# Convolutions placed 100 instructions sooner, and the output's late products tile by tile, in a hybrid decoder layer

## The chip, the cores and the metric

The kernel runs on one core of a Trainium2 chip. A core has a matrix engine (TensorE, PE in the profile), a vector engine (VectorE, DVE), a scalar engine (ScalarE, ACT), a general engine (GpSimd, POOL), and queues that issue transfers (SyncE's, SP, among them). Each engine takes its instructions in the order in which the program lists them for it; semaphores make one engine wait for another. Matrix products are written to PSUM, a small memory that VectorE and ScalarE then read; the other operands lie in SBUF.

The metric is the device time of one execution in microseconds (us). The time before is 1002.07 us, the median of three runs (1002.04 to 1004.28).

## The reference

The program computes one layer on 512 tokens and 16 meta tokens (528 positions) of width 1024, in float32:

```python
u = rmsnorm(h, mix_norm_w[i])
proj = u @ w_in[i]                       # pool | z | xbc | dt | gates
...
y_pool = pool_mixer(u_pool, ...) @ w_pool_up[i]
y_ssd = mamba2_branch(z, xbc, dt_raw, ...) @ w_ssd_out[i]
h = h + (gate_pool * y_pool + gate_ssd * y_ssd) @ w_o[i]
v = rmsnorm(h, mlp_norm_w[i])
hid = jax.nn.relu(v @ w_ff1[i])
h = h + (hid * hid) @ w_ff2[i]
out = rmsnorm(h, final_norm_w)
```

The part that the change touches lies in `mamba2_branch`. A causal depthwise convolution of width 4, with bias and Silu, runs over xbc (4096 channels, 32 tiles of 128 channels):

```python
y = b
for k in range(CONV_WIDTH):
    y = y + xp[:, k:k + seqlen] * w[k]
xbc = jax.nn.silu(y)
```

Its result is split into x (2048 channels, 32 heads), B and C (1024 each, 8 groups of 128 states). A chunked scan (chunks of 128) makes y per group from x, B, C and dt; y is multiplied by silu(z), normed per group, and multiplied by `w_ssd_out`.

## The kernel before

Every matrix product is made from a high and a low part of each operand: high times high, high times low, low times high, summed in PSUM. A weight block (128 x 1024) is loaded to `raw`, cast to its high part `whi` on ScalarE (line 111), and its low part `wlo` is the difference, made on VectorE (line 113). These go through pools of four buffers for `whi` and `wlo`.

The scan runs over eight groups g = 0 to 7. `ssd(g)` is a generator that makes the scan of group g in steps; `group_proj(g + 1)` is a generator that makes the projections of the next group: two tiles for B and C (`bt`, `ct`), two for x (`xc`), and z. `weave` takes a step of the one and a step of the other in turn, and between them steps of some side work. For group 7 there is no next group; its partner is `out_part`, which makes the middle part of the output product: for each of 8 output tiles d, the terms k = 8 to 13 of `w_ssd_out` (y of groups 4 to 6).

The steps of `ssd(g)`: transposes of B and x, the scaled x (`xdt`, `xdd`) and the decay matrix `abc` (subtract on ScalarE, line 638, and VectorE, line 641; Exp on ScalarE, lines 644 and 645); then C times B, its mask (`cbm`, line 658), the chunk states (`st`, lines 667 to 673) and the product of mask and decay (line 676); then for each half of the channels `po` (line 685) and `py` (line 691), and y on VectorE (lines 694 to 698); then the squares, their sums (`png`, lines 709 and 710), the root and its reciprocal (lines 712 and 714), and y in high and low parts (`yh`, `yl`, lines 718 to 722).

The convolution of a channel tile is `conv(dst, src, ct)`: one ScalarE instruction (bias and the weight of the newest position, line 437), three VectorE instructions (the three older positions, line 440), then Silu on ScalarE (line 442). For most tiles `src` is the PSUM tile `px` that the projection has just written (lines 215 and 218); for the x tiles of groups 4 to 7 it is a pair of SBUF tiles. PSUM tiles of this size (`px`, `pz`, `pgp`, `pso`, `psp`) come from one pool with two buffers; a tile can be taken when the last reader of the one two places before is done.

The order of instructions on each engine isn't written out by hand. A planner takes, whenever an engine is free in its model, the ready instruction with the smallest place; the place is the position in the trace of the Python program, and `tc.high_priority(100)` lets a block of instructions count as 100 places earlier. Before the change it is used for weight blocks (`block`, `pair_operands`). Buffers are given out in the same walk.

In `out_part`, `part` makes the products of one tile d for some k, and `add` copies the PSUM tile to SBUF (ScalarE, line 868) and adds it to `acc_d` in DRAM with a transfer issued by GpSimd (line 869). The staging tile comes from a pool of two buffers. Tiles d = 0 and 1 get k = 8 to 11 first; their k = 12 and 13 (y of group 6, not ready as early) come later, in three rounds over both tiles (line 880). Then the tiles d = 2 to 7 follow, each whole. `weight_sums_at` issues transfers on GpSimd that are paced by small copies (`seen`, line 797).

After the scan, `pool_pair` multiplies by pool weights (line 998, its copies at lines 1004 to 1014), the merge and the MLP follow (lines 1077 to 1670).

Of the kernel before, what the change touches and what calls it, by code (L numbers as in the profile page):

```python
# [11 lines left out]
AF = mybir.ActivationFunctionType  # L12
ALU = mybir.AluOpType
# [21 lines left out]
V_MIX, V_BG, V_PS, V_CW, V_CB, V_DS, V_SN, V_MN, V_DTB, V_AL = (  # L35
    0, 8, 24, 32, 160, 192, 208, 224, 232, 233)
# [28 lines left out]
def kernel(ctx: ExitStack, tc, xT, x, w, fx, f1, f2, vec, fnw, out):  # L65
    nc = tc.nc
    act, dve, pe, pool = nc.scalar, nc.vector, nc.tensor, nc.gpsimd
# [19 lines left out]
    def block_tiles():  # L87
        b = nblk[0]
        nblk[0] += 1
        return (b, raw_tile(f"raw{b}"),  # L90
                wp.tile([P, 1024], F32R, tag="whi", name=f"whi{b}"),
                wp.tile([P, 1024], F32R, tag="wlo", name=f"wlo{b}"))

    def block_load(t, c):
        nc.sync.dma_start(t[1][:, c], w[t[0], :, c])
# [5 lines left out]
    def after(*ins):  # L101
        st = ExitStack()
        for i in ins:
            if i is not None:
                st.enter_context(tc.issue_after(i.ins))
        return st
# [36 lines left out]
    def mm3s(ps, pairs, first=True, last=True):  # L143

        for n, ((ah, al), (bh, bl)) in enumerate(pairs):
            pe.matmul(ps, ah, bh, start=first and n == 0, stop=False)  # L146
            pe.matmul(ps, ah, bl, start=False, stop=False)
        for n, ((ah, al), (bh, bl)) in enumerate(pairs):
            pe.matmul(ps, al, bh, start=False, stop=last and n == len(pairs) - 1)
# [16 lines left out]
    def col(off, i, n=P):  # L166
        return vs[:n, off + i : off + i + 1]
# [25 lines left out]
    def psum2(name):  # L193
        return psa.tile([P, 1024], F32, tag="mm", name=name)

    def psum1(name):
        return psb.tile([P, 512], F32, tag="s", name=name)
# [150 lines left out]
    for t, name in ((rsh, "dgh"), (rsl, "dgl")):  # L348
        d = pre.tile([NT, 6, NT], F32R, tag="sq", name=name, bufs=2)
# [16 lines left out]
    def dtile(name):  # L366
        return dp.tile([P, W], F32, name=name)

    v, e, s, s2, pl, dt, acs = (dtile(n) for n in ("dv", "de", "ds", "ds2", "dpl", "ddt", "dacs"))
# [21 lines left out]
    for c in (slice(0, P), slice(P, W)):  # L391
        n = c.stop - c.start
# [41 lines left out]
    def conv(dst, src, ct):  # L434
        n = dst.shape[-1]
        e = src.shape[-1] - n
        act.activation(dst, src[:, e:], AF.Identity, bias=col(V_CB, ct), scale=col(V_CW, ct * 4 + 3))
        for j in range(1, 4):
            o = max(0, j - e)
            dve.scalar_tensor_tensor(dst[:, o:], src[:, e + o - j : e + n - j],  # L440
                                     col(V_CW, ct * 4 + 3 - j), dst[:, o:], op0=ALU.mult, op1=ALU.add)
        silu = act.activation(dst, dst, AF.Silu)
        mark[0] = dst[:, :1]
        if ct < 16:
            x_ready[ct // 2] = silu
# [84 lines left out]
    def group_proj(g, cur, gate=None):  # L530
# [4 lines left out]
        def plain(dst, t, skip):  # L535
            if first and (dst is bt or dst is ct):
                view = viewB if dst is bt else viewC
            else:
                runs, view = wide(psum2(f"px{g}_{t}"), skip)
                proj(runs, block(), X if first else U)  # L540
            conv(dst, first_raw(t, view, skip) if first else view, t)
# [205 lines left out]
    def staged(name):  # L747
        return gtp.tile([P, SEQ], F32, tag="gt", name=name)
# [90 lines left out]
    def out_part():  # L839

        def get(n):
            t = block_tiles()
            block_load(t, slice(0, 1024))

            with after(b_meta[G - 1] if n == 1 else None):
                cast = act.copy(t[2], t[1])
            if n == 1:
                late_cast[0] = cast
            with tc.issue_after(x_decayed[G - 1].ins) if n == 1 else nullcontext():
                dve.tensor_tensor(t[3], t[1], t[2].bitcast(F32), op=ALU.subtract)  # L850
            return t

        def pieces():
            blocks = [get(0), get(1)]
            for n in range(6):
                t = blocks[n] if n < 2 else get(n)
                for j in range(NK):
                    c = slice(j * P, (j + 1) * P)
                    yield t[2][:, c], t[3][:, c]

        un = pieces()

        def part(ps, d, ks):
            mm3s(ps, [(next(un), ys[k]) for k in ks], ks[0] == 8, ks[-1] == 13)

        def add(ps, d):
            o = staged(f"sp{d}")
            act.copy(o, ps)
            nc.gpsimd.dma_start(acc_d[d], o, accum_op=ALU.add)


        ps = [psum2(f"psp{d}")[:, :SEQ] for d in range(2)]
        for d in range(2):
            part(ps[d], d, range(8, 12))
            yield
        late = [[(next(un), ys[k]) for k in (12, 13)] for d in range(2)]
        for o in ((0, 0), (1, 0), (0, 1)):
            for d in range(2):
                for n, (a, b) in enumerate(late[d]):
                    pe.matmul(ps[d], a[o[0]], b[o[1]], start=False, stop=o[1] == 1 and n == 1)  # L880
            yield
        for d in range(2):
            add(ps[d], d)
        for d in range(2, NK):
            ps = psum2(f"psp{d}")[:, :SEQ]
            part(ps, d, range(8, 14))
            add(ps, d)
            yield
# [39 lines left out]
    for g in range(G):  # L928
        nxt = group_tiles(g + 1) if g + 1 < G else None
        fill = [group_proj(g + 1, nxt, GATE_AT.get(g))] if nxt else [out_part()]  # L930
        if g == 4:
            fill = [out_half()] + fill
        weave(ssd(g, cur), fill, 2 if g == 4 else 1, weight_sums_at(SETS_AT[g], PIECES.get(g, 12)),
              [sums_of_u(g)] if g in SUMS_AT else [])
        cur = nxt
# [115 lines left out]
    for d in range(NK):  # L1051
        ps = psum1(f"psl{d}")
# [108 lines left out]
    for n, d in enumerate(MERGE):  # L1161
# [9 lines left out]
        ps = psum2(f"pup{d}")[:, :SEQ]  # L1171
# [389 lines left out]
    for c in range(NC - 1):  # L1561
        z, e = c == 0, c == NC - 2

        n = 2 * c + 3
# [78 lines left out]
    for t in range(4):  # L1643
        T, st = t // 2, slice((t % 2) * P, (t % 2 + 1) * P)
        n = 0
        for half in range(2):
            parts = [(0, 512)] if half == 0 or t < 3 else [(0, 256), (256, 256)]
            for a, m in parts:
                ps = p2v[t] if T == 0 and half == 0 else lastp[:, 512:] if a else (
                    lastp[:, :512] if (t, half) == (3, 0) else psum1(f"pl{t}_{half}"))  # L1650
                ps = ps[:, a : a + m]
# [15 lines left out]
                src = ps  # L1667
                if not a:
                    src = ht[:, t, cs]
# [162 lines left out]
```

## Time and profile before

| | before |
|---|---|
| median of 3 runs | 1002.07 us (1002.04 to 1004.28) |
| the profiled execution, its own time | 1003.26 us |
| its span | 1001.6 us |
| granted TensorE clock | 0.999 |
| busy: TensorE, weight loads, VectorE, ScalarE, GpSimd | 989.0, 873.4, 804.2, 602.9, 121.9 us |

The span runs from the first to the last instruction of one profiled execution. In a row of a group or of a timeline stand: the start in us (timeline) and the duration, the engine (PEld is TensorE's load of a stationary operand, a name with q its queue), the line of the program, the operation, the tiles written and read, the shape, and in brackets or behind the bar the idle time of the engine just before, with what ended it. A timeline merges neighbours (x8 is eight of them). In a row of stretches stand the stretch, its length and the busy time of PE, PEld, DVE, ACT and POOL with the number of instructions, then the granted clock, the share of the DMA engines and GB/s. The ends of matmuls are modelled: one of 512 columns is shown as 0.39 us, though the next can start 0.23 us after it.

### The profile page before, as it was taken

Reading aid. Unit: us, or ns where it says so; the run is one execution under the profiler, and the core shown is the slowest. Engines: PE = TensorE matmul, PEld = TensorE weight load, DVE = VectorE, ACT = ScalarE, POOL = GpSimd, SP = SyncE. Lnnn points to the kernel's source line nnn. Section 1 sums busy time; section 2 is a strip of 40 time slices with the busy share of each in tenths; the row PEclk is TensorE's granted clock in tenths of the full one; section 3 lists DMA queues with packets and bytes.
Section 4 is the critical chain, followed back from the end, with each engine's and each line's share of the span. In section 5 each row is a group of like instructions: output and inputs, shape, how many; then the busy total and the mean of one; then the engine's idle time right before and its main releaser. Section 6 shows DMA issues by size and latency. Waiting matters only on the chain.

```text
span 1001.6 us, 15673 instructions
## 1 busy us (share of the span) xinstructions
PE 989.0 (99%) x6035; PEld 873.4 (87%) x6035; DVE 804.2 (80%) x1162; ACT 602.9 (60%) x855; POOL 121.9 (12%) x215
## 2 busy tenths in 40 slices
PE   9999999999999999999999999999999999999997
PEld 7889898989889999978898888888889999999986
DVE  7977997879855888978789667876988878888885
ACT  7657749494924658574345443377666666656654
POOL 0010321211212312223200001121000000000000
PEclk9999999999999999999999999999999999999999
DMA  7374868676798849678823732889354464454332
GB/s 245 89 254 140 265 182 238 195 192 199 221 262 265 232 122 278 211 161 172 286 68 127 252 101 77 259 232 323 88 197 149 142 194 138 157 185 151 129 106 84
DMA packets 61803, 184.52 MB, mean 184 GB/s; under 512 B 7072, under 2 KB 8416, under 8 KB 60704
## 3 DMA queue, kind: packets, MB, share of 16 engines
q1 hardware_dynamic: 39456, 109.00, 33.3%
q0 software_dynamic: 18240, 67.51, 26.4%
q10 hardware_dynamic: 4032, 7.00, 1.9%
q8 instruction: 47, 0.77, 0.3%
q14 instruction: 28, 0.23, 0.1%
HBM read 173.13 MB, written 58.59 MB: 231 GB/s over the span
## 4 chain that ended last, share of the span: by engine, by line
PE 84%; DVE 7%; ACT 4%; DMA 3%; issue 1%; SPq 0%; ACTq 0%; DVEq 0%
PE px L1451 8%; PE px L215 7%; PE alpha L1519 6%; PE pz L215 6%; PE px L1454 4%; PE px L218 4%; PE pgp L215 3%; PE alpha L1522 3%; PE pz L218 3%; PE pgs L215 3%; DMA raw<-in_w 2%; PE pqx L506 2%; PE py L691 2%; PE pgp L218 2%; PE pso L146 1%; PE wo_alpha L1213 1%
## 5 line engine op out<-in xcount | busy, mean ns | idle before, releaser
L113 DVE TENSOR_TENSOR wlo<-raw,whi 128x1024 fp32r<-128x1024 f32 (+2 forms) x88 | 102.2, 1171 | 45.0 <-ACT whi L111 29.7
L111 ACT CAST whi<-raw 128x1024 fp32r<-128x1024 f32 (+2 forms) x88 | 87.2, 1012 | 64.0 <-DMA raw<-in_w 15.8
L215 PE MATMUL px<-uh,whi 128*128 128x264 f32 (+1 forms) x320 | 81.1, 291 | 0.0
L218 PE MATMUL px<-ul,whi 128*128 128x264 f32 (+1 forms) x320 | 78.7, 284 | 0.0
L1226 DVE TENSOR_TENSOR ht<-ht,alpha 128x1024 f32<-128x1024 f32 x35 | 42.7, 1220 | 29.1 <-PE alpha L1519 29.1
L215 PEld LDWEIGHTS px<-uh,whi 128*128 128x128 f32 x320 | 60.5, 189 | 1.1 <-issue 0.9
L1149 ACT CAST shi<-rawf 128x1024 fp32r<-128x1024 f32 x42 | 44.2, 1053 | 28.0 <-PE alpha L1522 18.4
L218 PEld LDWEIGHTS px<-ul,whi 128*128 128x128 f32 x320 | 60.2, 188 | 0.4 <-issue 0.2
L1519 PE MATMUL alpha<-shi,hh 128*128 128x512 f32 x140 | 55.3, 395 | 0.7 <-DVE ht L1226 0.6
L1522 PE MATMUL alpha<-shi,hl 128*128 128x512 f32 x140 | 54.7, 391 | 0.0
L1150 DVE TENSOR_TENSOR slo<-rawf,shi 128x1024 fp32r<-128x1024 f32 x42 | 51.2, 1219 | 0.6 <-ACT shi L1149 0.6
L1454 PE MATMUL px<-vsl,shi 128*128 128x256 f32 x192 | 47.4, 280 | 0.0
L1451 PE MATMUL px<-vsh,shi 128*128 128x256 f32 x192 | 47.4, 281 | 0.0
L215 PE MATMUL pz<-uh,whi 128*128 128x512 f32 x112 | 43.8, 391 | 1.7 <-DVE xc L440 1.7
L218 PE MATMUL pz<-ul,whi 128*128 128x512 f32 x112 | 43.6, 390 | 0.0
L215 PE MATMUL px<-uh,wlo 128*128 128x264 f32 (+1 forms) x320 | 42.0, 283 | 0.0
L215 PEld LDWEIGHTS px<-uh,wlo 128*128 128x128 f32 x320 | 40.0, 188 | 0.0
L1519 PE MATMUL alpha<-slo,hh 128*128 128x512 f32 x140 | 37.4, 389 | 0.0
L1451 PEld LDWEIGHTS px<-vsh,shi 128*128 128x128 f32 x192 | 36.2, 188 | 0.9
L1454 PEld LDWEIGHTS px<-vsl,shi 128*128 128x128 f32 x192 | 36.1, 188 | 0.9
L1454 PE MATMUL px<-vl,shi 128*128 128x256 f32 x144 | 36.1, 283 | 0.0
L1451 PE MATMUL px<-vh,shi 128*128 128x256 f32 x144 | 36.0, 282 | 0.0
(599 smaller groups left out, 3068.3 us busy)
## 6 DMA issues: line engine op xcount, KB each, us to landing
raw<-in_w SPq DMA_DIRECT2D x96, 512.0 KB, 4.6
f_t<-in_f POOLq DMA_DIRECT2D x38, 512.0 KB, 7.5
f_s<-in_f POOLq DMA_DIRECT2D x26, 512.0 KB, 7.0
b<-in_f SPq DMA_DIRECT2D x21, 512.0 KB, 4.4
rawf<-in_f SPq DMA_DIRECT2D x36, 256.0 KB, 3.0
rawf<-f_t SPq DMA_DIRECT2D x36, 256.0 KB, 3.1
abc<-acs_d POOLq DMA_DIRECT2D x8, 1024.0 KB, 8.3
f_t<-f_t POOLq DMA_DIRECT2D x12, 512.0 KB, 6.7
```

What stands on the lines that cost most here:

```text
L111: act.copy(hi[:, c], raw[:, c])
L113: dve.tensor_tensor(lo[:, c], raw[:, c], hi[:, c].bitcast(F32), op=ALU.subtract)
L215: pe.matmul(o, wt, rhs[0][k][:, c], start=part == 0 and k == 0, stop=part == 1 and k == NK - 1)
L218: mm[0] = pe.matmul(o, wt, rhs[1][k][:, c], start=False, stop=False)
L506: at = pe.matmul(o, wk, f[k][0], start=start and not low and k == 0, stop=stop and low == 1 and k == 3, skip_group_check=True)
L1149: splits.append((act.copy(hi, src), dve.tensor_tensor(lo, src, hi.bitcast(F32), op=ALU.subtract)))
L1150: dve.tensor_tensor(lo, src, hi.bitcast(F32), op=ALU.subtract)))
L1226: added[0] = dve.tensor_tensor(o, o, src, op=op)
L1451: pe.matmul(ps, m, f[k][0], start=start and not low and k == 0, stop=stop and low == 1 and k == 3, skip_group_check=True)
L1454: pe.matmul(ps, m, f[k][1], start=False, stop=False, skip_group_check=True)
L1519: pe.matmul(ps[t], hh[:, p, seg, st], m, start=bool(first and not low and p == 0), stop=bool(last and low and p == 1), skip_group_check=True)
L1522: pe.matmul(ps[t], hl[:, p, seg, st], m, start=False, stop=False, skip_group_check=True)
```

## The change

Two edits. In `conv`, the ScalarE instruction and the three VectorE instructions stand in a block that counts as 100 places earlier; the Silu stays outside. In `out_part`, the late products run tile by tile instead of round by round: the six matmuls of tile 0, then its copy and its transfer in a block of 100 places earlier, a yield, then the same for tile 1. There are two yields where there were three, and the copies of both tiles no longer stand ahead of the step of tile 2.

```diff
     def conv(dst, src, ct):
         n = dst.shape[-1]
         e = src.shape[-1] - n
-        act.activation(dst, src[:, e:], AF.Identity, bias=col(V_CB, ct), scale=col(V_CW, ct * 4 + 3))
-        for j in range(1, 4):
-            o = max(0, j - e)
-            dve.scalar_tensor_tensor(dst[:, o:], src[:, e + o - j : e + n - j],
-                                     col(V_CW, ct * 4 + 3 - j), dst[:, o:], op0=ALU.mult, op1=ALU.add)
+        with tc.high_priority(100):
+            act.activation(dst, src[:, e:], AF.Identity, bias=col(V_CB, ct), scale=col(V_CW, ct * 4 + 3))
+            for j in range(1, 4):
+                o = max(0, j - e)
+                dve.scalar_tensor_tensor(dst[:, o:], src[:, e + o - j : e + n - j],
+                                         col(V_CW, ct * 4 + 3 - j), dst[:, o:], op0=ALU.mult, op1=ALU.add)
         silu = act.activation(dst, dst, AF.Silu)
...
         late = [[(next(un), ys[k]) for k in (12, 13)] for d in range(2)]
-        for o in ((0, 0), (1, 0), (0, 1)):
-            for d in range(2):
+        for d in range(2):
+            for o in ((0, 0), (1, 0), (0, 1)):
                 for n, (a, b) in enumerate(late[d]):
                     pe.matmul(ps[d], a[o[0]], b[o[1]], start=False, stop=o[1] == 1 and n == 1)
+            with tc.high_priority(100):
+                add(ps[d], d)
             yield
-        for d in range(2):
-            add(ps[d], d)
         for d in range(2, NK):
             ps = psum2(f"psp{d}")[:, :SEQ]
             part(ps, d, range(8, 14))
```

## The prediction

> **What bounds the kernel now.** I read the page first (engines, chain of waits, costliest groups), then busy time in stretches, then the groups of TensorE kept apart by shape, and last the timelines around the two places they name.
>
> ```profile
> span 1001.6 us, 15673 instructions
> ...
> PE 989.0 (99%) x6035; PEld 873.4 (87%) x6035; DVE 804.2 (80%) x1162; ACT 602.9 (60%) x855; POOL 121.9 (12%) x215
> ...
> PE 84%; DVE 7%; ACT 4%; DMA 3%; issue 1%; SPq 0%; ACTq 0%; DVEq 0%
> ...
> L215 PE MATMUL pz<-uh,whi 128*128 128x512 f32 x112 | 43.8, 391 | 1.7 <-DVE xc L440 1.7
> ```
> ```profile
> L146 PE MATMUL psp<-yh,whi 128*128 128x512 f32 x44 | 17.5, 397 | 1.4 <-ACT sp L868 1.4
> ```
> ```profile
> 60.00:110.00 50.00, 48.31 (x339) 43.93 (x338) 38.41 (x63) 29.72 (x42) 7.61 (x16) 1.00 0.66 220
> 110.00:315.00 205.00, 205.00 (x1330) 183.07 (x1329) 160.37 (x246) 134.65 (x182) 44.68 (x81) 1.00 0.77 219
> 315.00:430.00 115.00, 114.88 (x833) 106.62 (x832) 93.60 (x143) 72.84 (x104) 28.23 (x49) 1.00 0.73 211
> 430.00:450.00 20.00, 18.33 (x104) 14.61 (x103) 17.72 (x31) 17.27 (x26) 3.27 (x5) 1.00 0.66 163
> 450.00:500.00 50.00, 49.60 (x272) 42.61 (x271) 39.88 (x56) 21.60 (x29) 16.05 (x25) 1.00 0.86 230
> ```
>
> TensorE is busy 989.0 of 1001.6 us, and 84% of the chain of waits is its own work. So the change can win only what TensorE loses. Between 60 and 500 us that is 50 - 48.31 = 1.69, then 0.00, 0.12, 1.67 and 0.40 us, 3.88 in all. Two places hold 3.1 of it, and both have a name in the groups: the z product waits 1.7 us for the last step of a convolution (L440), and the output part waits 1.4 us for a copy out of PSUM (L868). These are the two helpers that the diff touches. VectorE stands at 80% of the span, and at 17.72 of 20 us around the second place, so whatever is put ahead there pushes something else back.
>
> **The first stall.** The rows come from the timelines of TensorE, ScalarE and VectorE.
>
> ```profile
> 101.35 2.09 PE L215 MATMUL px<-uh,wlo 128*128 128x264 f32 x16
> 105.13 0.47 PE L215 MATMUL pz<-uh,whi 128*128 128x512 f32 x1 [1.69 <-DVE xc L440]
> 108.88 1.98 PE L215 MATMUL pz<-uh,wlo 128*128 128x512 f32 x8
> ```
> ```profile
> 95.32 0.79 ACT L437 ACTIVATE xc<-px,vs 128x528 f32<-128x528 f32 x1
> ...
> 101.59 1.05 ACT L111 CAST whi<-raw 128x1024 fp32r<-128x1024 f32 x1 [1.58 <-PE px L218]
> ```
> ```profile
> 95.90 1.22 DVE L113 TENSOR_TENSOR wlo<-raw,whi 128x1024 fp32r<-128x1024 f32 x1
> ...
> 101.14 0.76 DVE L440 SCALAR_TENSOR_TENSOR xc<-px,vs,xc 128x527 f32<-128x527 f32 x1
> 101.82 1.22 DVE L113 TENSOR_TENSOR wlo<-raw,whi 128x1024 fp32r<-128x1024 f32 x1
> 102.95 0.76 DVE L440 SCALAR_TENSOR_TENSOR xc<-px,vs,xc 128x526 f32<-128x526 f32 x1
> ...
> 104.23 0.76 DVE L440 SCALAR_TENSOR_TENSOR xc<-px,vs,xc 128x525 f32<-128x525 f32 x1
> ```
>
> Two PSUM tiles serve px and pz in turn. pz takes the one that the first xc convolution reads. ScalarE had begun that convolution at 95.32, yet VectorE came to its three steps only at 101.14 to 104.99: 5.0 us after the ScalarE step ended at 96.11, behind scan work and weight splits with a better place in the queue. The diff gives the four instructions of a convolution the place of 100 instructions earlier. One px step traces 3 instructions of a weight block, 48 matmuls and 5 of the convolution, 56 in all, and a scan step some 16 to 40; so a convolution passes its own product and about one scan step. In all 32 convolutions move, 32 ScalarE and 96 VectorE instructions; no DMA, no wait, no instruction is added. The three steps take 3 x 0.68 = 2.0 us back to back (101.14 to 101.82 is one step), so started at 96.11 they end near 98.5 even with one 1.22 us split between. pz then follows px at px's pace: 16 matmuls in 2.09 us with a last one of 0.28 us are one each 0.121 us, so pz would be issued at 101.35 + 16 x 0.121 = 103.28 and not at 105.13. **Gain 1.85 us** (the 1.69 shown as idle leaves out the modelled tail of the last matmul).
>
> What is pushed back is at most 2.0 us late for each convolution: y products (L694 to L698), states, masks and splits. The weights have cover. The cast at 101.59 waits for TensorE to release a buffer, so casts run as far ahead as four buffers allow, and the split at 95.90, by count the one of this pz, is used at 108.88, 11.8 us later. Without that cover a split behind a convolution costs TensorE up to 2.0 us. From 110 to 430 us there is 0.12 us to win, so the other 30 convolutions are costed at nothing; the scan that hides them has its limits below, as a rival. The bounds of this term are -1.85 and, with one cover gone, +0.15.
>
> **The second stall.** Again the three timelines, and two rows of GpSimd and of the copies' transfers.
>
> ```profile
> 440.78 1.27 PE L880 MATMUL psp<-yh,whi 128*128 128x512 f32 x4
> 441.88 0.62 PE L880 MATMUL psp<-yh,wlo 128*128 128x512 f32 x2
> 442.74 0.49 PE L685 MATMUL po<-ct,st 128*128 128x128 f32 x2 [0.23 <-ACT st L667]
> 442.98 0.71 PE L880 MATMUL psp<-yh,wlo 128*128 128x512 f32 x2
> 443.53 1.09 PE L880 MATMUL psp<-yl,whi 128*128 128x512 f32 x4
> 446.06 0.50 PE L146 MATMUL psp<-yh,whi 128*128 128x512 f32 x1 [1.44 <-ACT sp L868]
> ```
> ```profile
> 442.58 1.06 ACT L644 ACTIVATE abc<-abc 128x1024 f32<-128x1024 f32 x1
> 443.54 1.04 ACT L846 CAST whi<-raw 128x1024 fp32r<-128x1024 f32 x1
> 444.49 1.05 ACT L645 ACTIVATE abc<-abc 128x1024 f32<-128x1024 f32 x1
> 445.44 1.05 ACT L868 COPY sp<-psp 128x512 f32<-128x512 f32 x2
> ```
> ```profile
> 446.31 1.80 POOL L869 DMA_DIRECT2D acc_d<-sp  x2 [9.50 <-ACT sp L868]
> ...
> 454.31 0.84 POOL L869 DMA_DIRECT2D acc_d<-sp  x1 [6.21 <-ACT sp L868]
> ...
> DMA to landing us min/median/max: 3.9/5.7/9.3
> ```
>
> The twelve late matmuls finish both tiles together, 443.53 to 444.62, and the two copies stand behind an Exp on ScalarE. So psp2, which needs a released PSUM tile, waits until 446.06. By the diff the six of tile 0 come first. Given their inputs they take 6 x 0.227 = 1.36 us (0.227 being 1.09 less a last 0.39, over three steps); tile 1's six then cover 1.36 us, and a copy lasts 0.59. With the copy placed ahead of the Exp or behind one, tile 0 is released between 443.2 and 444.2 and tile 1's six end near 443.9. psp2 was due at 443.53 + 4 x 0.227 = 444.44 and came at 446.06: **1.6 us, of which I take 1.4**, 0.2 staying for a copy that finds ScalarE in a 1.05 us instruction. Bounds: -1.6, and 0 if both copies stay behind the Exp.
>
> The Exp and the cast on ScalarE come up to 2 x 0.5 us later, and the second mask on VectorE with them, but by then TensorE has psp2's matmuls to run. The two transfers issued on GpSimd move too; that queue had stood idle 9.50 us before them, so they pass nothing, and the third copy's staging buffer, free when the first transfer lands (446.31 + 5.7 = 452.0 before the third is issued at 454.31), is free sooner. One yield goes from the loop, so psp2 to psp7 are traced one scan step sooner; the scan's two y steps are still ahead of psp2.
>
> **Does the lead last?** The stretch behind must be sooner as well.
>
> ```profile
> 475.93 6.25 DMA raw<-in_w
> 482.28 1.05 ACT whi L111
> ```
>
> In the chain of waits a weight block lands at 482.18 and its cast is behind it. Its buffer is released by a split that follows the last group's y, whose last products follow TensorE's own order; so I let this chain move with TensorE.
>
> **The sum.** 1001.6 - 1.85 - 1.4 = 998.35 us of span. The profiled run itself took 1003.26 us, which is 1.66 around its span, but the median of the runs is 1002.07, 0.47 above the span. Moved from the median, -3.25 gives 998.8 us.
>
> [...] The page has this row among ScalarE's groups:
>
> ```profile
> L442 ACT ACT_TABLE_LOAD x10 | 12.8, 1283 | 3.2 <-DVE bt L440 3.1
> ```
>
> The 32 Silus behind the convolutions share 10 loads of 1.283 us. Ready sooner, a Silu can fall among a scan's Exps and bring two loads in front of a mask. [...]
>
> **The rivals.** (1) The second gain is taken back: the block that lands at 482.18 doesn't come sooner, TensorE waits longer for it, and only 1.85 stays: 1002.07 - 1.85 = 1000.2. For it speaks the 6.25 us transfer in the chain; against it that its trigger follows TensorE.
>
> (2) Slower: convolutions ahead of masks and states. The rows are of groups 6 and 2.
>
> ```profile
> 403.53 2.29 DVE L676 TENSOR_TENSOR abc<-abc,cbm 128x2048 f32<-128x2048 f32 x1
> ```
> ```profile
> 405.92 1.09 PE py L691 x16
> ```
> ```profile
> 174.53 2.29 DVE L676 TENSOR_TENSOR abc<-abc,cbm 128x2048 f32<-128x2048 f32 x1 [0.31 <-ACT abc L645]
> ```
> ```profile
> 181.36 0.87 PE L691 MATMUL py<-abc,xdt 128*64 128x128 f32 x10
> ```
>
> py follows its mask by 0.1 us in group 6 and by 4.5 in group 2. Two convolutions (bt, ct) in front of a mask are 4.0 us: covered in group 2, 3.9 us lost in group 6, and about as much in any other group with no margin. Two such groups make 7.8: 998.8 + 7.8 = 1006.6. It decides from 6.3 us on (3.25 + 3.0). Against it: bt's convolution already stands ahead of the mask in group 6, and TensorE has px to run meanwhile.
>
> (3) Table loads: two more loads in front of a mask in two groups without margin, 4 x 1.283 = 5.1 us: 998.8 + 5.1 = 1003.9. Against it: a Silu keeps its old place in the order and yields to Exps that are ready.
>
> (4) The edit does nothing, because both stalls were planned that way and merely get other names: 1002.07.
>
> **How the numbers follow.** About 0.3% (3.0 us, so 999.1 and 1005.1) is what a measurement of this kernel can tell from no change. Forecast 0.60, with its own range 997.2 to 1000.0: 0.49 of it beyond 999.1, 0.11 within. Rival 1: 0.10, within. Rival 2: 0.18, slower. Rival 3: 0.08, 0.04 of it slower. Rival 4: 0.04. Faster 0.49, within 0.29, slower 0.22. The lower end takes in the 0.23 and 0.40 us of small waits at 442.74 and after 450 and some of those later on; the upper end reaches to rival 2: 997.0 to 1006.6.
>
> **What would show it.** Right: the z product no longer waits for L440, psp no longer waits for L868; TensorE idles under 0.3 us in the stretch to 110 and under 0.6 us in the 20 us around the copies; pz of group 1 begins near 103.3. Rival 1: the wait for L1010 or for a weight cast behind the copies grows by 1 us or more. Rival 2: TensorE idles before py or po, released by L676 or L673. Rival 3: more than 10 loads at L442. The forecast is wrong if either named stall stays, or if a new wait of TensorE between 60 and 500 us is over 1 us.

## The result and the profile after

The changed kernel takes 1009.04 us (median of 6 runs, 1008.11 to 1012.58), the kernel before on the same chip 1002.79. The ratio is 1.0062 (95% interval 1.0046 to 1.0078): slower by 6 us, where 998.8 was forecast and 1006.6 was the upper end. The profiled execution took 1008.36 us, its span is 1006.7. Behind the edit the lines of the changed kernel have moved by one: L440 is L441, L868 is L869, L1010 is L1011.

First the lines that answer to those of before: from the page of the changed kernel (span, busy time, two groups), from its groups by shape, and its five stretches.

```profile
span 1006.7 us, 15668 instructions
...
PE 989.8 (98%) x6035; PEld 874.6 (87%) x6035; DVE 804.6 (80%) x1162; ACT 604.3 (60%) x857; POOL 127.5 (13%) x215
...
L215 PE MATMUL pz<-uh,whi 128*128 128x512 f32 x112 | 43.8, 391 | 0.0
```
```profile
L146 PE MATMUL psp<-yh,whi 128*128 128x512 f32 x44 | 17.3, 394 | 0.0
```
```profile
60.00:110.00 50.00, 50.00 (x351) 45.73 (x350) 37.27 (x61) 27.74 (x40) 6.59 (x14) 1.00 0.67 218
110.00:315.00 205.00, 201.96 (x1319) 180.68 (x1318) 161.03 (x248) 136.78 (x183) 53.69 (x83) 1.00 0.78 219
315.00:430.00 115.00, 114.12 (x830) 105.78 (x830) 94.96 (x143) 74.97 (x107) 24.67 (x46) 1.00 0.71 210
430.00:450.00 20.00, 19.79 (x112) 16.02 (x111) 16.46 (x29) 17.63 (x27) 4.56 (x10) 1.00 0.78 177
450.00:500.00 50.00, 44.98 (x243) 38.59 (x242) 35.35 (x49) 18.54 (x26) 15.95 (x25) 0.97 0.80 210
```

Both named stalls are gone: the z product and psp wait for nothing, and the stretches to 110 and from 430 to 450 lost their 1.69 and 1.46 us. But 110 to 315, which had no idle time, has 3.04 us, and 450 to 500 has 5.02 where it had 0.40. The idle time of the five stretches went from 3.88 to 0.00 + 3.04 + 0.88 + 0.21 + 5.02 = 9.15 us. That is +5.27 of idle time, and the span grew by 5.1. The granted clock of the last stretch is 0.97 and no longer 1.00.

TensorE's timeline of the changed kernel has three waits behind the new numbers (start, duration; in brackets the idle time before and what ended it):

```profile
150.11 1.98 PE L215 MATMUL pgp<-uh,wlo 128*128 128x512 f32 x8
155.12 0.50 PE L710 MATMUL png<-qhg,ones_r 128*128 128x512 f32 x1 [3.04 <-ACT qhg L330]
...
479.52 0.39 PE L999 MATMUL pxx<-t0h,whiS 128*128 128x264 f32 x1 [1.18 <-ACT pu L1005]
...
488.03 0.39 PE L999 MATMUL pz<-t1h,whiB 128*128 128x264 f32 x1 [3.85 <-ACT pu L1011]
```

**The stall at 152.** VectorE's timeline of the changed kernel, then one line of before:

```profile
147.50 0.77 DVE L441 SCALAR_TENSOR_TENSOR xc<-px,vs,xc 128x527 f32<-128x527 f32 x1 [1.00 <-ACT xc L438]
148.18 0.68 DVE L696 TENSOR_TENSOR yt<-yt,py 128x512 f32<-128x512 f32 x1
...
150.79 0.68 DVE L699 TENSOR_TENSOR yt<-yt,zt 128x512 f32<-128x512 f32 x1
```
```profile
147.58 0.68 DVE L698 TENSOR_TENSOR yt<-yt,zt 128x512 f32<-128x512 f32 x1
```

A step of the convolution of x tile 5 now stands ahead of group 1's y. It is not ready: VectorE waits 1.00 us for the ScalarE step, with the y step of 148.18 behind it. The last product of y starts 3.21 us later than before. ScalarE turns that into the 3 us (changed kernel, then before):

```profile
151.51 1.05 ACT L704 ACTIVATE sqg<-yt 128x1024 f32<-128x1024 f32 x1
152.58 1.28 ACT L757 ACT_TABLE_LOAD   x1
153.88 0.69 ACT L757 ACTIVATE gp<-pgp,vs 128x512 f32<-128x512 f32 x1
154.46 0.61 ACT L330 CAST qhg<-sqg 128x512 fp32r<-128x512 f32 x1
...
471.45 0.59 ACT L869 COPY sp<-psp 128x512 f32<-128x512 f32 x1 [3.54 <-PE psp L149]
471.93 1.14 ACT L722 CAST yh<-yt 128x512 fp32r<-128x512 f32 x2
...
486.65 1.04 ACT L111 CAST whi<-raw 128x1024 fp32r<-128x1024 f32 x1 [4.97 <-DMA raw<-in_w]
487.60 0.37 ACT L1011 COPY pu<-pz 128x264 f32<-128x264 f32 x1
```
```profile
151.49 0.62 ACT L330 CAST qhg<-sqg 128x512 fp32r<-128x512 f32 x1 [1.29 <-DVE sqg L704]
...
468.52 1.28 ACT L721 CAST yh<-yt 128x512 fp32r<-128x512 f32 x2
```

The squares come late, so the gate's table load and its sigmoid, which need nothing of them, pass `qhg`: it starts at 154.46 where it started at 151.49. TensorE has run out of pgp by then.

**The stall at 484.** The lower rows of the same two fences show it. The cast of 486.65 waits 4.97 us for its weight block, and the 0.37 us copy of z stands behind it in ScalarE's queue. TensorE needs that copy, not the cast. In the kernel before the cast started at 482.28, and TensorE lost 0.40 us in the whole stretch. The block is 4.37 us later, and most of that is its buffer, which comes free later: `yh` is cast at 471.93 and no longer at 468.52, behind a copy `sp` that waits 3.54 us for TensorE (y itself, line 718 of before, starts only 1.54 us later), and the splits on VectorE follow it. By the times, the last reader of the buffer is the split `wloD`: SyncE's queue issues the block 0.03 us after its end. VectorE and SyncE's queue, in the changed kernel and in the one before:

```profile
477.76 1.23 DVE L133 TENSOR_TENSOR wloD<-raw,whiD 128x1024 fp32r<-128x1024 f32 x1 [0.20 <-ACT whiD L132]
...
479.02 2.06 SPq L95 DMA_DIRECT2D raw<-in_w  x3
```
```profile
474.68 1.22 DVE L133 TENSOR_TENSOR wloD<-raw,whiD 128x1024 fp32r<-128x1024 f32 x1
...
475.93 5.17 SPq L95 DMA_DIRECT2D raw<-in_w  x3
```

Three blocks are issued, the first of them 3.09 us later, and within 2.06 us instead of 5.17. In the chain of waits the first lands 7.54 us after its issue (6.25 before). So 3.09 us of the delay are the buffer and 1.29 the transfer. That the three hold one another up on the DMA engines is likely but not shown.

**The clock.** Single microseconds behind that wait, in the changed kernel (granted clock: third number from the end):

```profile
488.00:489.00 1.00, 0.97 (x6) 0.97 (x7) 1.00 (x2) 0.00 (x0) 0.00 (x0) 0.74 1.03 393
489.00:490.00 1.00, 1.00 (x6) 1.00 (x6) 0.29 (x1) 0.15 (x1) 0.00 (x0) 0.50 1.03 389
...
491.00:492.00 1.00, 1.00 (x7) 1.00 (x7) 0.93 (x3) 0.00 (x0) 0.00 (x0) 0.56 0.98 373
```

After the wait TensorE runs at half clock for about 3.5 us. It counts as busy there, so the idle time doesn't show it.

### The profile page after: what moved, and what is told of

The parts are those of the page before. It is cut to its first block, busy times and chain, and to the rows that moved or that the text cites. A ratio compares the mean times of both kernels' runs of the same rounds, so it can differ in the third digit from the quotient of the medians.

```text
span 1006.7 us, 15668 instructions
## 1 busy us (share of the span) xinstructions
PE 989.8 (98%) x6035; PEld 874.6 (87%) x6035; DVE 804.6 (80%) x1162; ACT 604.3 (60%) x857; POOL 127.5 (13%) x215
## 4 chain that ended last, share of the span: by engine, by line
PE 89%; ACT 4%; DVE 4%; DMA 2%; issue 1%; SPq 0%; ACTq 0%; DVEq 0%
PE px L1452 8%; PE px L215 7%; PE alpha L1520 6%; PE pz L215 6%; PE px L1455 4%; PE px L218 3%; PE alpha L1523 3%; PE pz L218 3%; PE pgp L215 3%; PE pgs L215 3%; PE py L692 2%; PE pqx L507 2%; PE pso L146 1%; PE wo_alpha L1214 1%; PE po L686 1%; PE pf L147 1%
```

## The experiments

Each median is of 4 to 12 runs. All ratios are against the kernel before, run on the same chip; its median was 1002.6 to 1002.8 us in each set of runs.

| kernel | median, us | ratio (95% interval) |
|---|---|---|
| conv_alone | 1005.11 | 1.0021 (1.0007 to 1.0035) |
| late_alone | 1007.84 | 1.0048 (1.0033 to 1.0063) |
| conv5_behind_y | 1006.73 | 1.0046 (1.0028 to 1.0064) |
| copies_behind_y | 1011.71 | 1.0089 (1.0074 to 1.0104) |
| late_z_first | 1002.64 | 1.0001 (0.9991 to 1.0011) |
| after_z_first | 1005.23 | 1.0026 (1.0011 to 1.0040) |
| rounds_prio | 1005.13 | 1.0025 (1.0015 to 1.0035) |
| x1_only | 1004.06 | 1.0009 (0.9999 to 1.0019) |
| x1_late_z | 1002.41 | 0.9995 (0.9986 to 1.0004) |
| late_m_late | 1007.89 | 1.0051 (1.0037 to 1.0065) |
| before_m_late | 1002.83 | 0.9997 (0.9987 to 1.0007) |
| conv5_m_late | 1007.37 | 1.0046 (1.0030 to 1.0062) |
| late_no_sets | 1007.09 | 1.0040 (1.0028 to 1.0052) |
| before_no_sets | 1002.39 | 0.9997 (0.9988 to 1.0006) |
| all_four | 1003.53 | 1.0006 (0.9995 to 1.0017) |
| all_no_sets | 1001.63 | 0.9991 (0.9979 to 1.0003) |
| conv_alone_5 | 1003.28 | 1.0003 (0.9992 to 1.0015) |
| conv_alone_5_z | 1002.52 | 0.9990 (0.9979 to 1.0001) |

### Each edit alone

Each kernel has one hunk of the change and leaves the other as it was before.

> The first edit alone, the output part as before. Theory (two new queues: y of group 1 behind a convolution on VectorE, and copies of the output tiles ahead of y's casts on ScalarE; the first belongs to this edit): the z wait of 1.7 us goes, the wait for the cast of the squares near 152 us (3.0 us) is there, the 1.4 us for the copy near 445 stays, and the waits for L1005 and L1011 near 480 are back at under 0.6 us; span 1001.6 - 1.85 + 3.6 = about 1003.4. Rival (TensorE's lead as such runs into the weight block near 482, whichever edit gives the lead): the wait near 484 grows here too, to 2 us or more, and the span is 1005 or more.

> The second edit alone, the convolutions as before. Theory: the z wait of 1.7 us near 105 is back, no wait near 152, the copy's 1.4 us is gone, and the waits for L1005 and L1011 near 480 are there, 1 and 3 to 4 us, with a lower clock behind them: span 1001.6 - 1.6 + 1.3 + 3.4 + 1 = about 1005.7. Rival (both stretches suffer only from both edits together, or from the lead): the waits near 480 stay under 1.5 us in sum and the span is about 1000.

Each edit alone is slower, and each makes its own stall. conv_alone has the 3.04 us wait near 152 and only 0.81 us at z's copy near 480; late_alone has no wait near 152, and 1.17 and 4.28 us at the two copies near 480. So the convolutions make the first stall and the late products the second. conv_alone alone doesn't rule out that a mere lead makes the second, since its TensorE reaches pxx 5.16 us later than before (480.97 for 475.81): its profiled execution is the slowest of its ten (1009.70 us), with the clock halved behind two waits (last section). conv_alone_5 below has the lead and no such stall.

### The stall at 152: the convolution of tile 5 behind y

```diff
+                with after(y_done[1] if ct == 5 else None):
                     dve.scalar_tensor_tensor(dst[:, o:], src[:, e + o - j : e + n - j],
                                              col(V_CW, ct * 4 + 3 - j), dst[:, o:], op0=ALU.mult, op1=ALU.add)
```

`after` orders the three steps behind the last product of group 1's y (`y_done`); the rest is the changed kernel.

> The changed kernel, with the three VectorE steps of one convolution (the second x tile of group 2) put behind the last product of group 1's y. Theory (this one convolution, in front of y with the engine waiting for ScalarE's step, makes the squares late): the wait near 152 falls from 3.0 to under 1 us: span about 1003.5 to 1004, the waits near 480 as in the changed kernel. Rival (y is late because of the other convolutions, the sums of u or the Silu and gate on ScalarE): the wait stays at 2 us or more and the span within 1 us of 1006.7.

VectorE's and TensorE's timelines of this kernel:

```profile
147.36 0.69 DVE L700 TENSOR_TENSOR yt<-yt,zt 128x512 f32<-128x512 f32 x1
147.97 1.56 DVE L442 SCALAR_TENSOR_TENSOR xc<-px,vs,xc 128x527 f32<-128x527 f32 x2
```
```profile
151.38 0.40 PE L711 MATMUL png<-qhg,ones_r 128*128 128x512 f32 x1
```

y ends where it did before, and png starts with no wait. The stall goes with the order of three instructions, and the time falls by 2.3 us against the changed kernel's 1009.04. In this profile the half clock behind z's copy lasted about twice as long as in the changed kernel's (granted clock 0.50 from 484 to 490 and 0.79 to 491; there 0.50 from 489 to 491, with 0.74 before and 0.56 behind).

### A repair that moved the wait: the copies behind y's casts

```diff
-            act.copy(o, ps)
+            with after({4: halved, 6: y_cast}[d][G - 1] if d in (4, 6) else None):
+                act.copy(o, ps)
```

The changed kernel, with the copies of output tiles 4 and 6 behind `qhg` and `yh` of group 7 as they were before the change.

> The changed kernel, with two copies put back behind group 7's y on ScalarE: that of tile 4 behind the cast of the squares, that of tile 6 behind the casts of y. Nothing else is set. Theory (the copies' place on ScalarE makes y late, so the buffer of the weight block comes free late): y's casts start 3 us sooner, the block lands 3 us or more sooner, the waits for L1005 and L1011 fall to under 1.5 us in sum, no lower clock: span 1006.7 - 5 = about 1001.7, the 3.0 us near 152 still there. Rival (the block is late because TensorE is early and its transfer shares the DMA engines with the accumulations): the wait for L1011 stays at 3 us or more and the span is within 1 us of 1006.7.

My theory fell: 1011.71 us. VectorE and TensorE in this kernel:

```profile
490.40 1.23 DVE L113 TENSOR_TENSOR wlo<-raw,whi 128x1024 fp32r<-128x1024 f32 x1 [7.85 <-ACT whi L111]
491.55 0.42 DVE L1015 TENSOR_TENSOR pu<-pu,pxx 128x264 f32<-128x264 f32 x1
```
```profile
492.02 0.59 PE L1001 MATMUL pxx<-uh,whiD 128*128 128x264 f32 x1 [5.43 <-DVE pu L1015]
```

Here z's copy stood ahead of the cast, and the wait at it was gone. But on VectorE the block's split, which needs the cast, stood ahead of the addition that releases pxx. The block itself came later still: its cast began at 489.33. But `yh` was cast at 471.96, no sooner than in the changed kernel, so this kernel doesn't tell whether an earlier `yh` would make the block earlier. The late block cost TensorE what was small and ready behind it in both kernels: 3.85 us at z's copy in the changed one, 5.43 us at the addition here.

### The stall at 484: the late block's cast and split behind z

```diff
-        while True:
-            hi, lo = block()
+        for n in range(64):
+            hi, lo = block(*((z_add[POOL_ORDER[0]], copied[POOL_ORDER[0]]) if n == 1 else ()))
```

The second block of the output's last part gets its cast behind the copy of z and its split behind the addition of z (`z_add`). late_z_first does it to late_alone, after_z_first to the whole change.

> The edit of the late products alone, and in addition the second weight block of the output's last part has its cast placed behind the copy of z on ScalarE and its split behind the addition of z on VectorE; nothing is left out. Theory (TensorE's wait of 4.4 us at 482 is the copy of z standing behind a cast whose transfer is late; nobody needs the cast itself yet): that wait is under 0.5 us, granted clock 1.00 from 484 to 492, the late block is not waited for afterwards, and the time falls by 4 us and some 1 us of clock from 1007.8 to about 1003 us. Rival (the block itself is needed by then): the wait moves to the products of psl 4 that read the block, 3 us or more, and the time stays over 1006.5 us.

> The whole change, with the second weight block's cast and split of the output's last part behind z's copy and addition, and nothing else. Theory (that head of the line costs 3.85 us of wait and the halved clock in the changed kernel too): 1009.0 - 5 = 1004 us, no wait over 1.5 us between 477 and 492, and the stall of some 3 us near 155 stays. Rival (with both parts of the change the block itself is needed): a wait of 3 us or more before 492 and over 1006.5 us.

ScalarE in late_z_first:

```profile
481.31 0.38 ACT L1010 COPY pu<-pz 128x264 f32<-128x264 f32 x1 [1.07 <-PE pz L998]
...
484.71 1.05 ACT L111 CAST whi<-raw 128x1024 fp32r<-128x1024 f32 x1 [3.02 <-DVE pu L1014]
```

late_alone's 1007.84 became 1002.64, and the whole change's 1009.04 became 1005.23. No wait over 1.5 us is left between 477 and 492, and the clock stays at 1.00 from 482 to 498. Against late_alone the wait of 4.28 us is gone, and with it the half clock behind it, 5.2 us together. The blocks come hardly sooner (casts at 484.71, 488.75 and 491.16, in late_alone 485.30, 488.84 and 491.48; the first of these casts now also stands behind z's addition, and in the chain of waits its block lands at 484.63, in late_alone at 485.19), but nothing that TensorE needs stands behind them.

### Which part of each edit does it

rounds_prio keeps the three rounds of before and gives only the two copies the priority; x1_only is the kernel before with the priority for the convolutions of tiles 2 and 3 alone; x1_late_z adds the late products and z's order to it.

```diff
-        for d in range(2):
-            add(ps[d], d)
+        with tc.high_priority(100):
+            for d in range(2):
+                add(ps[d], d)
...
-        with tc.high_priority(100):
+        with tc.high_priority(100) if ct in (2, 3) else nullcontext():
```

> The output's middle part keeps its three rounds over both tiles, and only the two copies and their DMAs get the priority of 100 instructions; convolutions as before. Theory (what costs in the edit is the lead of 1.5 us with the copies of sp 4 and sp 6 ahead of the casts of group 7's y, which comes from the tile-by-tile order with its third yield, not from the priority): here sp 6 stays behind the casts, so the waits near 476 and 482 are under 1.5 us each, no halved clock behind them, and the time is between 1001.2 and 1003.5 us. Rival (any lead of TensorE's here comes back at the weight block): the wait for psp 2 is gone, but the one for z's copy is 3 us or more and the time is over 1005 us.

> Only the convolutions of group 1's two x tiles (ct 2 and 3) are placed with the priority of 100 instructions sooner; all other convolutions and the output's middle part are as before. Theory (the first gain of 1.85 us was real and independent of the 30 other convolutions, which alone make the wait near 152): z of group 1 does not wait for the conv, no wait of TensorE over 1 us near 152, the copy wait of 1.6 us near 446 stays, and the time is 1002.6 - 1.85 = 1000.8 us. Rival (an earlier TensorE only meets the next late product sooner, so that a lead cannot be kept): a new wait of 1 to 2 us between 103 and 160 and a time within 0.5 us of before's.

> The priority for group 1's two x convolutions alone, the edit of the late products, and the late weight block's cast and split behind z's copy and addition; nothing is left out. Theory (the two first gains stand once both stalls that they made are taken away): 1002.6 - 1.85 - 1.6 + 1.3 for the wait at the copy of pxx = about 1000.5 us, between 1000 and 1002. Rival (the lead is given back at a next place): 1003 us or more with a new wait of 2 us or more behind 490.

All three went the rival's way or near it. TensorE in rounds_prio, then in x1_only:

```profile
444.69 0.49 PE L146 MATMUL psp<-yh,whi 128*128 128x512 f32 x1 [0.49 <-ACT sp L868]
...
485.00 0.59 PE L999 MATMUL pz<-t1h,whiB 128*128 128x264 f32 x1 [3.29 <-ACT pu L1011]
```
```profile
98.62 0.36 PE L215 MATMUL px<-uh,whi 128*128 128x264 f32 x1 [1.67 <-DVE xc L441]
```

In rounds_prio the wait for the copy falls from 1.44 to 0.49 us, the casts of `yh` stand where they did before the change, and the wait at z's copy is 3.29 us all the same. Its first block is issued at 475.91, as before (475.93), but TensorE reaches pxx 1.56 us sooner (474.25 for 475.81) and the block's cast starts 1.34 us later (483.62 for 482.28; the transfer takes 7.61 us). With the 0.40 us of before these make the 3.29. So neither the `sp` copies ahead of `yh` nor a late buffer is needed for the stall at 484; a lead that is gained beside group 7 brings it. In x1_only the 1.7 us wait only moved from pz to the px product ahead of it. VectorE's timeline there has the last step of ct's convolution at 98.73, so that the other PSUM tile was still held. x1_late_z keeps this wait (1.67 us) and gains a new one of 1.57 us at psl.

### Why the block is late

Two suspects share the DMA engines with the blocks: the loads `m<-gate_d` (256 KB each, issued from 480.6 us on in late_alone, first used at 561 us), and the weight sums that run beside group 7.

```diff
+            behind = pool.tensor_copy(seen, acc[NK - 1][:, :1])
             for d in MERGE:
-                with tc.issue_after(mixed[0].ins):
+                with tc.issue_after(behind.ins):
...
-SETS_AT = {0: 1, 1: 1, 2: 2, 3: 1, 4: 2, 5: 2, 6: 1, 7: 1}
+SETS_AT = {0: 1, 1: 1, 2: 2, 3: 1, 4: 2, 5: 2, 6: 1, 7: 0}
```

> The edit of the late products alone, with the seven loads m<-gate_d (256 KB each, first used at 561 us) held on POOL until VectorE's last addition of psl, so that they no longer run beside the second weight block; nothing is left out. Theory (the block is late because the DMA engines are full from 474 to 492, and in the changed kernel these loads start at 480.6 instead of mostly at 487 and later): the block's transfer falls from about 8.1 to 6.3 us, the wait of 4.4 us at 482 falls to about 2.5 us, the clock behind it stays at 1.00, and the time is 1007.8 - 2 - 1 = about 1005 us. Rival (the block is late because its buffer comes free late, and the transfer's length does not depend on these loads): the wait stays over 4 us and the time within 0.7 us of 1007.8.

> The kernel before with the same seven loads held until the last addition of psl; convolutions and late products as before. Theory (in the kernel before the loads already start after the block has landed, all but one): no change over 0.5 us, 1002.2 to 1003.1 us. Rival (the stretch is bound by the DMA engines in the kernel before too): the wait of 0.55 us at z and others go, 1001.5 us or less.

> The whole change with the conv of x tile 5 behind group 1's last y product (as in the run that did that alone, 1006.7 us), and the seven m<-gate_d loads held as above. Theory (transfer): the wait for z's copy falls by about 2 us and the halved clock behind it goes, 1006.7 - 3 = about 1003.7 us. Rival (buffer): over 1006 us.

> The edit of the late products alone, with the weight sums that run on the DMA queue of POOL beside group 7 made later, with the others that are left to the end (nothing is left out; the order on the other engines is the same). Theory (the DMA engines are full from 440 on, and this backlog makes the block of 482 late): the block's cast starts at least 1.5 us sooner than 485.3, the wait of 4.4 us for z's copy falls under 3 us, and the time is 1006 us or less. Rival (the block is late only because the cast and split ahead of it release its buffer late, and because three blocks are then issued at once): the cast within 1 us of 485.3 and the time within 0.8 us of 1007.8.

> The kernel before with the same weight sums made later; nothing is left out. Theory (backlog): the weight block's cast at 482.28 starts sooner, z's wait of 0.55 us goes, and the time is between 1001.7 and 1002.6 us, unless the later sums cost on their side. Rival: 1002.4 to 1003 us.

Neither suspect is the cause by itself. Without the loads beside it the block's cast began 1.0 us sooner (484.30 for 485.30 in late_alone), without the sums 1.3 us sooner, 0.9 of it against TensorE's own place. The waits were still 3.02 and 3.39 us, the clock still fell to 0.50 behind them, and the times stayed within 0.8 us of late_alone's. In late_no_sets the DMA engines were busy for 0.45 of the time from 460 to 470, and from 474 to 478 they were busy for 0.98 again: the three blocks and the reloads of `acc` fill them by themselves. conv5_m_late kept a wait of 4.52 us. Holding the loads even went with a transfer that was shorter in one pair (6.71 us for late_alone's 7.95) and longer in the other (8.21 for 6.85 in conv5_behind_y). What remains is the buffer that comes free late, and a longer transfer whose cause stays open. Blocks issued close together are one suspect, but x1_only issues them over 5.16 us, as before, and its first still takes 7.20 us. No run tried an additional buffer.

### Is a lead kept?

all_four is the whole change with tile 5 behind y, the m loads held, the first block's cast behind the first copy of pxx, and the second block's cast and split behind z; all_no_sets adds the later sums. conv_alone_5 is the first edit alone with tile 5 behind y, conv_alone_5_z adds z's order.

```diff
-            hi, lo = block()
+            hi, lo = block(*((None, c_copy[POOL_ORDER[0]]), (z_add[POOL_ORDER[0]], copied[POOL_ORDER[0]]))[n] if n < 2 else ())
```

> The whole change; the conv of x tile 5 behind group 1's last y product; the m<-gate_d loads held; the first weight block's cast behind the first copy of pxx, and the second block's cast and split behind z's copy and addition. Nothing is left out. Theory (the gains of 1.85 and 1.6 us stand once the three stalls that they made are gone): no wait over 1 us after the first stage, 1002.6 - 1.85 - 1.6 - 0.5 for z's wait of before = about 998.7 us, 997.5 to 1000. Rival (the lead is given back at a next place, as in the two kernels with the priority for two convolutions only): a new wait of 1.5 us or more and a time over 1000.5 us.

> The kernel with all four repairs (1003.5 us), with the same weight sums made later. Theory (from 474 to 497 the blocks' arrival, by full DMA engines, sets when TensorE ends the products psl, so that a lead of 2.8 us on arrival was given back; with less on the DMA engines the blocks come sooner): psl ends at 496 us of the span or sooner, the time is between 999.5 and 1002 us. Rival (VectorE's splits, pooling and additions set that end): psl ends within 0.5 us of 497.7 and the time stays within 0.8 us of 1003.5.

> All convolutions with the priority (the first edit alone), and the three steps of x tile 5 behind group 1's last y product; the late products as before. Theory (the first edit's gain of 1.85 us stands once the stall near 155 is gone, since the chain from y to the weight blocks of 482 moves with TensorE there): no wait over 1 us from 60 to 440, psl ends about 1.5 us sooner in the span than in the kernel before, and the time is 1002.7 - 1.85 + 0.4 = about 1001.2 us. Rival (any lead is given back by 497, by full DMA engines): psl ends within 0.5 us of 497.35 and the time is 1002.3 us or more.

> The same with the second weight block's cast and split behind z's copy and addition. Theory: z's wait goes too, about 1000.7 us, below both kernels. Rival (psl waits for VectorE's additions, as in the kernels with a lead of 2.8 us): 1002 us or more.

The wlo products of the output's last part (psl), from TensorE's instructions on that tile: in before, the changed kernel, and all_four (first and last start behind the durations):

```profile
L149 PE MATMUL psl<-yh,wlo x16: 389/389/397, 487.6 to 497.4; 128*128 128x512 f32 x16
```
```profile
L149 PE MATMUL psl<-yh,wlo x16: 389/389/397, 493.5 to 503.3; 128*128 128x512 f32 x16
```
```profile
L149 PE MATMUL psl<-yh,wlo x16: 387/389/395, 484.6 to 497.7; 128*128 128x512 f32 x16
```

all_four enters psl 3.0 us ahead of the kernel before and leaves it 0.3 us behind. VectorE and TensorE in all_four:

```profile
492.18 2.35 DVE L113 TENSOR_TENSOR wlo<-raw,whi 128x1024 fp32r<-128x1024 f32 x2
...
495.67 0.68 DVE L1057 TENSOR_TENSOR acc<-acc,psl 128x512 f32<-128x512 f32 x1
```
```profile
496.40 0.50 PE L146 MATMUL psl<-yh,whi 128*128 128x512 f32 x1 [2.04 <-DVE acc L1057]
```

VectorE is busy without a gap from 490 to 498, as it was in the kernel before, with the splits of the late blocks, the pooling and the additions that release psl. So the lead is given back once more. With the sums taken away as well (all_no_sets), the blocks came 1.5 to 1.7 us sooner, psl ended at 496.0, and the time was 1001.63 us, as the theory of that run had it and the lowest median of all. So the arrival of the blocks, by way of their splits on VectorE, has a part in where the lead ends; but the interval against the kernel before still touches 1.

In conv_alone_5 the profiled execution did what the theory said: no wait over 0.7 us from 60 to 440, psl ended 1.1 us sooner (496.3 for 497.4), span 999.8 us. TensorE reached pxx, the first block was issued and its cast started 1.0 to 1.1 us sooner than before, and z's copy cost 0.47 us: this lead does carry the block with it. Its median is 1003.28 all the same, with runs from 1000.95 to 1005.12; the kernel before, in the same set, ran from 1001.61 to 1005.82. So no gain is shown for the first edit, even freed of its stall. conv_alone_5_z, at 0.9990 (0.9979 to 1.0001), is the nearest to one.

## Why the prediction was wrong

**The two gains were real, in their places.** pz of group 1 starts at 103.36 (forecast 103.28), psp waits for no copy, and idle times there are 0.00 and 0.21 us (bounds 0.3 and 0.6). The forecast named its own refutation, a new wait over 1 us between 60 and 500; there are three.

**First step that failed: "the other 30 convolutions are costed at nothing".** They cost the 3.04 us at 152. I took a stretch without idle time as one in which nothing could be won, and forgot that it is also one in which everything can be lost. I allowed each y product to come 2.0 us late, which is VectorE's own time for three steps; it came 3.21 us late, because the step that was put ahead was not ready itself and held the queue for 1.00 us besides. And I didn't ask whether anything on ScalarE would pass the late `qhg`; a table load and a sigmoid did. VectorE's share of the squares ends at 153.28 (0.69 us from 152.59), so they cost some 1.2 us of the three. conv5_behind_y shows the cause: three instructions reordered, 3.04 us gone. Rival 2 had the right kind of mechanism, a convolution ahead of scan work, but looked at masks and states (waits released by L676 or L673), where no new wait over 1 us came.

**Second step: "so I let this chain move with TensorE".** TensorE was 0.5 us ahead of before at pxx (475.29 for 475.81), and the block's cast was 4.4 us behind (486.65 for 482.28). The chain does move with TensorE where the lead is gained long before group 7, as in conv_alone_5. A lead that is gained beside group 7's y does not move it (in rounds_prio the block is issued at 475.91, for 475.93): there the chain hangs on the order in ScalarE's and VectorE's queues and on the transfers. So the step holds for the first edit and fails for the second. Rival 1 named the block and the wait for L1010. But it priced the wait at the gain taken back, 1.4 us; it was 1.18 + 3.85 us and half a clock behind it. The missing part was that a wait of the cast is passed on to whatever stands behind it: late_z_first removed 5.2 us with the blocks about as late as ever.

**Rival 3.** Two more table loads came (at L443, x11 for 10, and L646, 128.78 and 130.74 us), and TensorE has no wait there. The load in the stall at 152 is not an additional one; it merely moved ahead of `qhg`, from 154.58 to 152.58.

**The sum with what was measured:** -1.85 - 1.6 for the two stalls that went; +3.0 for the one at 152; +1.2 and +3.45 (3.85 less the 0.4 of before) for the two copies; +1.5 for the clock (from the start of pz to that of psl, 488.03 to 492.57, TensorE took 4.54 us, and 3.02 before): +5.7. The last wlo product of psl starts 5.9 us later than before (503.3 for 497.4); the span is 5.1 us longer, and where the last 0.8 was won back was not followed. The range failed because no rival had losses of two kinds at once.

What stays open: what lengthens the first block's transfer, and why the twelve runs of conv_alone_5 spread over 4 us although its profile keeps the gain. Part of that spread goes with the clock: its six runs up to 1002.5 us had a mean granted clock of 0.998 or 0.999, and four of its six above 1004 had 0.997. The wait of 1.46 us for the copy, which it still has, is a suspect (last section).

## What to carry to other kernels

A priority on a group of instructions doesn't only serve the one that was late. Look in each in-order queue at what a moved instruction now stands ahead of, and above all whether it is ready there: an instruction that waits at the head costs its wait as well as its duration (1.00 and 0.77 us at 147.50). Where a cast or split waits for a transfer, put the small copies and additions that release PSUM ahead of it (in late_z_first that took 5.2 us away). And before a gain early in the kernel is booked at the end, find the next stretch in which transfers or another engine set the pace; a lead may end there, as the 3.0 us of all_four did in psl.

## What the runs showed of the hardware

**The same idle time, three prices.** The wait at 152 was 3.04 us in the changed kernel, in conv_alone and in after_z_first. The stretch from 156 to 158 us in these three:

```profile
156.00:158.00 2.00, 2.00 (x11) 1.63 (x11) 1.94 (x2) 1.98 (x3) 1.32 (x2) 1.00 1.09 205
```
```profile
156.00:158.00 2.00, 2.00 (x7) 1.53 (x7) 1.85 (x2) 1.97 (x3) 0.75 (x1) 0.50 1.03 180
```
```profile
156.00:158.00 2.00, 2.00 (x6) 1.54 (x6) 1.93 (x2) 1.97 (x3) 0.84 (x1) 0.55 0.96 147
```

In the first the clock stayed at 1.00; in the second it was 0.50 from the first matmul on, for about 6 us; in the third it fell only 1.5 us after work had begun again, and stayed low for about 3 us. In eleven of twelve such idle times of 3.0 to 5.4 us in these profiles the clock was halved behind them. Behind one shorter wait it fell too. TensorE in conv_alone, at the copy that psp waits for, and the stretch behind it; then the stretch behind the same wait of 1.44 us in the kernel before:

```profile
449.64 0.50 PE L146 MATMUL psp<-yh,whi 128*128 128x512 f32 x1 [1.45 <-ACT sp L869]
...
451.00:453.00 2.00, 2.00 (x15) 1.67 (x16) 2.00 (x3) 0.97 (x2) 0.70 (x1) 0.50 0.90 110
```
```profile
447.00:449.00 2.00, 2.00 (x21) 1.71 (x22) 2.00 (x5) 1.38 (x2) 1.11 (x2) 1.00 0.68 83
```

conv_alone_5 has this wait as well, 1.46 us, and its profiled execution a mean clock of 0.999, as that of the kernel before has. Behind the 1.69 us at the z product in the kernel before (60 to 110) and the 2.04 us at psl in all_four (494 to 500) the clock stayed at 1.00. Added up over single microseconds, the drops behind the waits of 3.0 to 4.5 us took 1.7 us from the clock in two profiles (after_z_first and, behind its 3.85 us, the changed kernel) and 3.4 us in eight, which is 3.4 or 6.8 us at half speed. What decides whether and for how long the clock falls was not shown.

So the 3.04 us in conv_alone cost about twice their length, with the 3.4 us that the clock took behind them. The spread of the changed kernel's runs, 1008.1 to 1012.6, is of about that size, and so is that of the kernel before, 1001.6 to 1005.8, which has the wait of 1.44 us; that the one makes the other was not tried.

**One switch of the table** took 1.30 us on ScalarE at 152.58, from the load to the start of the sigmoid; the load itself is 1.28.
